# Second layer of the MLP: sixteen pairs in the seven block products, and row tiles finished as their products end

## The chip, the core and the metric

The kernel runs on one core of a Trainium2 chip. Its engines work side by side: TensorE (PE) multiplies matrices into the accumulators (PSUM), VectorE (DVE) and ScalarE (ACT) work element by element on PSUM and SBUF, GpSimd (POOL) does the same on SBUF, and SyncE (SP) issues the DMAs between SBUF and the chip's DRAM. Each engine takes its instructions in a fixed order and waits at semaphores. The metric is the time of one execution in device microseconds (us); lower is better.

## What is computed

One residual block over 1024 rows of 1024 columns: attention branches, and then an MLP with 4096 inner columns. The change lies in the MLP, and within it in the product with `w_down` and what follows.

```python
h = rms_norm(x, g_pre_mlp[l])
u = jnp.square(jax.nn.relu(h @ w_up[l]))
x = x + rms_norm(u @ w_down[l], g_post_mlp[l])
```

All values are float32. For precision each factor of a product is split into a high part in the engine's fp32r form (`hi`, a cast on ScalarE) and the rest (`lo`, a subtract on VectorE), and each block product is three matmuls: hi x hi, hi x lo, lo x hi.

## The kernel before

**First layer (up).** `up_pair(n)`, for n = 0 to 15, makes two 128-row tiles of the transposed hidden matrix, both halves of the rows, as four blocks u11, u12, u21, u22 of 128 x 512. It uses a seven-product scheme (a Strassen-Winograd form) instead of eight products. For the second layer it then builds on GpSimd the sums S1 = u12 + u22, S2 = S1 - u11, S3 = u11 - u12, S4 = u21 - S2 (lines 818 to 821), and stores A11 (u11), A12 (u21), A22 (u22) and S1 to S4 in DRAM, through SP's queue (line 826). For the last pair, n = 15, it builds no sums and stores the four plain blocks A11, A12, A22, A21.

**Second layer (down).** Again seven products stand for eight. `STORED` names their left factors in order: A11, S1, S2, A22, S3, S4, A12; the right factors are B11, T1, T2, T4, T3, B22, B21, where T1 = B12 - B11, T2 = B22 - T1, T4 = T2 - B21 and T3 = B22 - B12 are made on GpSimd by `sub` (line 862) from blocks of `w_down`. A product runs over PP = 8 pairs of inner tiles (`pp`), each with two entries `e`; pair 7 has only one (`entries`), since the 16th up pair is left out of the scheme. For a pair, `load_a` and `load_b` fetch the two factors, `parts_of` splits them (lines 607 and 608), and 24 matmuls (2 entries, 4 row tiles `t`, 3 terms) of line 898 add them into four banks. After the last pair each bank is added or copied into `lower[t]`, `upper[t]` or `p5s` (lines 902 to 924): `lower` becomes rows 0 to 3, `upper` rows 4 to 7.

**Last step.** The 16th up pair is then multiplied in the ordinary way for all eight row tiles (the `dn` matmuls of line 949, 12 for a tile). Each tile's two halves are added to its total (line 955), the tile's mean square is taken (line 108), 1 / root made by two small GpSimd operations (lines 114 or 116, and 117), the gain row `g_post2` multiplied (line 962, on GpSimd for six tiles and on VectorE for two), the residual `xf` added (line 965), and the two halves of the row are stored (line 966).

**Buffers and order.** Each tile has a tag with a fixed number of buffers; a new tile waits until an older one of its tag is no longer used. Four tags matter: `w` (four buffers of 128 x 1024, made by `wide`: u1 and u2 of an up pair, which hold u11, u12 and u21, u22; us12 and us34, which hold S1 to S4; and t1 of pairs 0 to 3, the differences T1, later T2), `row` (four; blocks of `w_down`, and before the change also the last step's `xf` and `of`), `page` (24; the hi and lo parts, four for a pair, so six pairs) and `big` (16; at first the split h blocks of the up layer, then the totals and t1 of pairs 4 to 7). A planner orders each engine's instructions ahead of the run, by program order and by when it reckons their inputs ready, so that loads and splits run ahead of PE as far as the buffers allow. PSUM has eight banks, two for each name in `BANKS`.

Of the kernel before, what the change touches and what calls it, by code (L numbers as in the profile page):

```python
# [41 lines left out]
def hybrid_block_kernel(  # L42
# [67 lines left out]
    def rstd_of(ms, pool, name):  # L110
# [22 lines left out]

    s_dram = {
        name: [dram.tile([P, 2, HALF], F32, name=f"s_dram{name}{i}") for i in range(NF // 4)]
        for name in ("A11", "A12", "A21", "A22", "S1", "S2", "S3", "S4")
    }
    bias_dram = dram.tile([N_DIFF, NREL], F32, name="bias_dram")
    bias_rows = dram.tile([N_DIFF, P, NREL], F32, name="bias_rows")
# [450 lines left out]
    def pair_page(name, dt=F32R):  # L590
        return page(name, [P, 2, HALF], dt)

    def wide(name, dt=F32):

        return stream.tile([P, 2, HALF], dt, tag="w", name=name, bufs=4)
# [10 lines left out]
    def split(hi, lo, raw):  # L606
        nc.scalar.copy(hi, raw)  # L607
        nc.vector.tensor_tensor(lo, raw, f32(hi), op=ALU.subtract)  # L608
# [159 lines left out]
    def up_pair(n):  # L768
# [43 lines left out]
        relu2(u21, u21)  # L812

        parts = {"A11": u11, "A12": u21, "A22": u22}
        if n < UP - 1:
            us12, us34 = wide(f"us12_{n}"), wide(f"us34_{n}")
            s1, s2, s3, s4 = us12[:, 0, :], us12[:, 1, :], us34[:, 0, :], us34[:, 1, :]
            nc.gpsimd.tensor_tensor(s1, u12, u22, op=ALU.add)  # L818
            nc.gpsimd.tensor_tensor(s2, s1, u11, op=ALU.subtract)
            nc.gpsimd.tensor_tensor(s3, u11, u12, op=ALU.subtract)  # L820
            nc.gpsimd.tensor_tensor(s4, u21, s2, op=ALU.subtract)
            parts |= {"S1": s1, "S2": s2, "S3": s3, "S4": s4}
        else:
            parts["A21"] = u12
        for name, part in parts.items():
            nc.sync.dma_start(out=s_dram[name][n // 2][:, n % 2, :], in_=part)

# [5 lines left out]


    PP = UP // 2
    wd = w_down.rearrange("(pp e j p) (k d) -> j k pp p e d", e=2, j=2, p=P, k=2)
    lower, upper, p5s, chain = [], [], [], []

    def entries(pp):
        return 2 if pp < PP - 1 else 1  # L840

    def load_a(name, pp):
        raw = raw_tile(f"{name}_{pp}", [P, 2, HALF])
        n = entries(pp)
        nc.sync.dma_start(out=raw[:, :n, :], in_=s_dram[name][pp][:, :n, :])
        return raw

    def load_b(j, k, pp, name):
        raw = row(f"b{j}{k}_{name}_{pp}", [P, 2, HALF])
        n = entries(pp)  # L850
        nc.sync.dma_start(out=raw[:, :n, :], in_=wd[j, k, pp, :, :n, :])
        return raw

    def parts_of(raw, name, pp):
        n = entries(pp)
        hi, lo = pair_page(f"{name}_hi{pp}"), pair_page(f"{name}_lo{pp}")
        split(hi[:, :n, :], lo[:, :n, :], raw[:, :n, :])
        return hi, lo

    def sub(out, in0, in1, pp):  # L860
        n = entries(pp)
        nc.gpsimd.tensor_tensor(out[:, :n, :], in0[:, :n, :], in1[:, :n, :], op=ALU.subtract)

    def right(name, pp):

        if name == "B11":
            b11, b12 = load_b(0, 0, pp, "a"), load_b(0, 1, pp, "a")
            t1 = wide(f"t1_{pp}") if pp < 4 else big.tile([P, 2, HALF], F32, tag="big", name=f"t1_{pp}")
            sub(t1, b12, b11, pp)
            chain.append(t1)  # L870
            return b11
        if name == "T1":
            return chain[pp]
        if name == "T2":
            sub(chain[pp], load_b(1, 1, pp, "b"), chain[pp], pp)
            return chain[pp]
        if name == "T4":
            b21 = load_b(1, 0, pp, "c")
            sub(b21, chain[pp], b21, pp)
            return b21  # L880
        if name == "T3":
            b22, b12 = load_b(1, 1, pp, "d"), load_b(0, 1, pp, "d")
            sub(b12, b22, b12, pp)
            return b12
        if name == "B22":
            return load_b(1, 1, pp, "e")
        return load_b(1, 0, pp, "f")

    for left, other in zip(STORED, ("B11", "T1", "T2", "T4", "T3", "B22", "B21")):
        accs = [bank(BANKS[t], f"d{left}_{t}") for t in range(4)]  # L890
        for pp in range(PP):
            a_hi, a_lo = parts_of(load_a(left, pp), f"l{left}", pp)
            b_hi, b_lo = parts_of(right(other, pp), f"r{other}", pp)
            for e in range(entries(pp)):
                for t in range(4):
                    ts = slice(t * P, (t + 1) * P)
                    for i, (st, mv) in enumerate(((a_hi, b_hi), (a_hi, b_lo), (a_lo, b_hi))):
                        nc.tensor.matmul(  # L898
                            accs[t], st[:, e, ts], mv[:, e, :],
                            start=(pp == 0 and e == 0 and i == 0), stop=(pp == PP - 1 and i == 2),  # L900
                        )
        for t in range(4):
            if left == "A11":
                lower.append(big.tile([P, 2, HALF], F32, tag="big", name=f"lower{t}"))
                nc.scalar.copy(lower[t][:, 0, :], accs[t])
            elif left == "S1":
                if t % 2 == 0:
                    p5s.append(big.tile([P, 2, HALF], F32, tag="big", name=f"p5_{t}"))
                nc.scalar.copy(p5s[t // 2][:, t % 2, :], accs[t])
            elif left == "S2":  # L910
                nc.vector.tensor_tensor(lower[t][:, 1, :], accs[t], lower[t][:, 0, :], op=ALU.add)
            elif left == "A22":
                upper.append(big.tile([P, 2, HALF], F32, tag="big", name=f"upper{t}"))
                nc.scalar.copy(upper[t][:, 0, :], accs[t])
            elif left == "S3":
                v, q, p4, p5 = lower[t][:, 1, :], upper[t][:, 1, :], upper[t][:, 0, :], p5s[t // 2][:, t % 2, :]
                nc.vector.tensor_tensor(q, accs[t], v, op=ALU.add)
                nc.gpsimd.tensor_tensor(p4, q, p4, op=ALU.subtract)
                nc.gpsimd.tensor_tensor(q, q, p5, op=ALU.add)
                nc.gpsimd.tensor_tensor(v, v, p5, op=ALU.add)  # L920
            elif left == "S4":
                nc.vector.tensor_tensor(lower[t][:, 1, :], accs[t], lower[t][:, 1, :], op=ALU.add)
            else:
                nc.vector.tensor_tensor(lower[t][:, 0, :], accs[t], lower[t][:, 0, :], op=ALU.add)


    g_post2 = load_row(2, big.tile([P, D], F32, tag="big", name="grow2"))
    last_a, last_b = [], []
    for j in range(2):
        raw = raw_tile(f"last_a{j}", [P, 2, HALF])  # L930
        for i in range(2):
            nc.sync.dma_start(out=raw[:, i, :], in_=s_dram[f"A{i + 1}{j + 1}"][PP - 1][:, 1, :])
        parts = pair_page(f"last_a_hi{j}"), pair_page(f"last_a_lo{j}")
        split(*parts, raw)
        last_a.append(parts)
        raw = row(f"last_b{j}", [P, 2, HALF])
        f = NF - 2 + j
        nc.sync.dma_start(out=raw, in_=w_down[f * P:(f + 1) * P, :].rearrange("p (k d) -> p k d", k=2))
        parts = pair_page(f"last_b_hi{j}"), pair_page(f"last_b_lo{j}")
        split(*parts, raw)  # L940
        last_b.append(parts)
    for i, t in enumerate((4, 5, 6, 7, 0, 1, 2, 3)):
        c, ts = t // 4, slice((t % 4) * P, (t % 4 + 1) * P)
        accs = [bank(BANKS[(2 * i + n) % 4], f"dn_{t}_{n}") for n in range(2)]
        for j in range(2):
            (a_hi, a_lo), (b_hi, b_lo) = last_a[j], last_b[j]
            for p, (st, mv) in enumerate(((a_hi, b_hi), (a_hi, b_lo), (a_lo, b_hi))):
                for n in range(2):
                    nc.tensor.matmul(  # L949
                        accs[n], st[:, c, ts], mv[:, n, :],  # L950
                        start=(j == 0 and p == 0), stop=(j == 1 and p == 2),
                    )
        tot = (upper if c else lower)[t % 4]
        for n in range(2):
            nc.vector.tensor_tensor(tot[:, n, :], accs[n], tot[:, n, :], op=ALU.add)
        tot = tot.rearrange("p a b -> p (a b)")
        xt, o = row(f"xf_{t}"), row(f"of_{t}")
        nc.sync.dma_start(out=xt, in_=x2_dram[t * P:(t + 1) * P, :])
        s2 = pb.tile([P, 1], F32, tag="ssq1", name=f"sf2_{t}", bufs=4)
        mean_square(tot, o, s2)  # L960
        r = rstd_of([s2], pb, f"f{t}")
        (nc.vector if i > 5 else nc.gpsimd).tensor_tensor(tot, tot, g_post2, op=ALU.mult)
        for n in range(2):
            ns = slice(n * HALF, (n + 1) * HALF)
            nc.vector.scalar_tensor_tensor(o[:, ns], tot[:, ns], r, xt[:, ns], op0=ALU.mult, op1=ALU.add)  # L965
            nc.sync.dma_start(out=out[t * P:(t + 1) * P, ns], in_=o[:, ns])


# [48 lines left out]
```

## Time and profile before

| | us |
|---|---|
| median of 3 runs (1511.29 to 1513.62) | 1512.61 |
| the profiled execution | 1511.9 |
| its span, first to last instruction | 1510.2 |
| PE busy | 1442.4 (96%) |
| VectorE busy | 950.0 (63%) |
| ScalarE busy | 740.0 (49%) |
| GpSimd busy | 421.2 (28%) |

The busy times are those of the profiled execution, as shares of its span. Matmuls overlap in the engine, and a busy PE is not PE at its peak: the spacing of the starts tells the rate. The granted clock of TensorE is given as a share of 2.4 GHz; 0.5 is its lower level, 1.2 GHz. The chain of waits follows the work that ended last back from the end, at each step to what released it. In a timeline, the time in brackets is how long the engine had stood idle, and what ended it.

### The profile page before, as it was taken

To read this page: it belongs to the slowest core of one execution; us is meant where nothing else is said; L and a number is where in the kernel's file an instruction comes from. 1 tells how busy PE (TensorE), PEld (TensorE's weight loads), DVE (VectorE), ACT (ScalarE), POOL (GpSimd) and SP (SyncE) were. 2 spreads that over 40 slices of the span, in tenths; PEclk is the share of its full clock that TensorE was granted. 3 is DMA by queue.
4 is the path that set the end of the run, shared out by engine and by line. 5 is a ranking of instruction groups with operands and counts; after the bars stand their busy time and mean duration, and the time that the engine had idled before them with its cause. 6 is when DMAs were issued, how large, how long until landed. Compare 5 with 4: busy or idle time off the path is not lost. (4 is left out here: it accounts for less than half of the span.)

```text
span 1510.2 us, 20192 instructions
## 1 busy us (share of the span) xinstructions
PE 1442.4 (96%) x7314; PEld 1224.7 (81%) x7314; DVE 950.0 (63%) x1384; ACT 740.0 (49%) x1326; POOL 421.2 (28%) x382
## 2 busy tenths in 40 slices
PE   7999999999999999999999749999999999999993
PEld 6888998898889888888888538788888888888882
DVE  5478988898687857445544464444444587556526
ACT  6456766665565545843334433454445345344311
POOL 2022322220000000000011256766654563434205
PEclk9999999999999999999999869999999999999997
DMA  5332223121332253644367534444446775677615
GB/s 199 88 117 65 69 54 87 56 67 57 105 84 64 77 195 112 216 140 167 112 197 222 187 104 155 153 163 158 160 156 212 251 249 169 206 243 245 201 41 195
DMA packets 94411, 218.93 MB, mean 145 GB/s; under 512 B 9340, under 2 KB 25960, under 8 KB 94312
## 3 DMA queue, kind: packets, MB, share of 16 engines
q1 hardware_dynamic: 94312, 217.66, 44.9%
q8 instruction: 57, 0.93, 0.3%
q14 instruction: 42, 0.34, 0.1%
HBM read 151.28 MB, written 60.31 MB: 140 GB/s over the span
## 5 line engine op out<-in xcount | busy, mean ns | idle before, releaser
L198 PE MATMUL acc_gate<-h_hi,lo_gate 128*128 128x512 f32 x256 | 101.0, 394 | 0.0
L196 PE MATMUL acc_gate<-h_hi,hi_gate 128*128 128x512 f32 x256 | 100.9, 394 | 0.0
L197 PE MATMUL acc_gate<-h_lo,hi_gate 128*128 128x512 f32 x256 | 100.8, 394 | 0.0
L331 DVE TENSOR_TENSOR_SCAN rest<-rest 128x896 f32<-128x896 f32 (+3 forms) x64 | 87.6, 1373 | 20.6 <-POOL rest L326 20.3
L608 DVE TENSOR_TENSOR w_lo<-ws,w_hi 128x1024 fp32r<-128x1024 f32 x32 | 44.9, 1405 | 73.6 <-ACT w_hi L607 64.2
L326 POOL TENSOR_SCALAR_AFFINE_SELECT rest<-rest 128x128 f32<-128x128 f32 x64 | 23.5, 368 | 240.7 <-ACT rest L322 236.3
L608 DVE TENSOR_TENSOR lS_lo<-raw_S,lS_hi 128x1024 fp32r<-128x1024 f32 (+1 forms) x32 | 51.7, 1616 | 38.3 <-ACT lS_hi L607 38.3
L116 POOL TENSOR_SCALAR rstd_o<-s 128x1 f32<-128x1 f32 x8 | 2.8, 354 | 249.1 <-DMA xr<-in_x_dram 211.7
L607 ACT CAST lS_hi<-raw_S 128x1024 fp32r<-128x1024 f32 (+1 forms) x32 | 32.0, 1001 | 79.4 <-DMA raw_S<-s_dramS 43.6
L898 PE MATMUL dS<-rT_hi,lS_lo 128*128 128x512 f32 x180 | 70.0, 389 | 0.0
L898 PE MATMUL dS<-rT_lo,lS_hi 128*128 128x512 f32 x180 | 70.0, 389 | 0.0
L898 PE MATMUL dS<-rT_hi,lS_hi 128*128 128x512 f32 x180 | 70.0, 389 | 0.0
L567 PE MATMUL mix<-y,hi_mix 128*128 128x512 f32 x256 | 68.6, 389 | 0.0
L607 ACT CAST w_hi<-ws 128x1024 fp32r<-128x1024 f32 x32 | 33.5, 1046 | 69.8 <-POOL ws L773 60.9
L394 ACT ACTIVATE s<-s,low 128x896 f32<-128x896 f32 (+7 forms) x64 | 49.7, 777 | 29.7 <-DVE low L389 29.5
L375 POOL MEMSET bias<- 64x64 f32 x4 | 0.6, 144 | 214.4 <-DMA bias<-bias_rows 214.4
L389 DVE CUSTOM_DVE_ANT_0 s<-z,bias 128x512 f32<-128x512 f32 (+3 forms) x64 | 37.0, 586 | 32.4 <-PE z L263 26.6
L723 ACT ACTIVATE u<-u 128x512 f32<-128x512 f32 x48 | 30.2, 630 | 54.8 <-DVE u L802 33.7
L567 PEld LDWEIGHTS mix<-y,hi_mix 128*128 128x128 f32 x256 | 48.0, 188 | 10.0
L198 PEld LDWEIGHTS acc_gate<-h_hi,lo_gate 128*128 128x128 f32 x256 | 48.2, 188 | 9.2
L197 PEld LDWEIGHTS acc_gate<-h_lo,hi_gate 128*128 128x128 f32 x256 | 48.2, 188 | 8.8
L608 DVE TENSOR_TENSOR lA_lo<-raw_A,lA_hi 128x1024 fp32r<-128x1024 f32 (+1 forms) x24 | 35.5, 1478 | 31.4 <-ACT lA_hi L607 30.9
(341 smaller groups left out, 4896.9 us busy)
## 6 DMA issues: line engine op xcount, KB each, us to landing
raw_up<-in_w_up_dram SPq DMA_DIRECT2D x32, 512.0 KB, 3.9
s_dramS<-us SPq DMA_DIRECT2D x60, 256.0 KB, 2.0
raw_S<-s_dramS SPq DMA_DIRECT2D x28, 512.0 KB, 4.5
s_dramA<-u SPq DMA_DIRECT2D x49, 256.0 KB, 3.1
raw_A<-s_dramA SPq DMA_DIRECT2D x21, 512.0 KB, 3.7
raw_gate<-in_w_in_dram SPq DMA_DIRECT2D x16, 512.0 KB, 3.7
gate_dram<-gt SPq DMA_DIRECT2D x32, 256.0 KB, 2.5
y<-y_dram SPq DMA_DIRECT2D x16, 512.0 KB, 6.1
```

The costliest lines, as they stand in the source:

```text
L196: nc.tensor.matmul(acc, w_hi[:, ks], h_hi[k][:, cs], start=(k == 0), stop=False)
L197: nc.tensor.matmul(acc, w_hi[:, ks], h_lo[k][:, cs], start=False, stop=False)
L198: nc.tensor.matmul(acc, w_lo[:, ks], h_hi[k][:, cs], start=False, stop=(k == NK - 1))
L326: nc.gpsimd.affine_select(tl[:, dg], tl[:, dg], pattern=[[-1, P]], compare_op=ALU.is_gt, fill=fill, base=0, channel_multiplier=1,)
L331: nc.vector.tensor_tensor_scan(back, back, back, 1.0, op0=ALU.mult, op1=ALU.bypass)
L389: nc.vector.tensor_tensor_reduce(out=s[:, c0:c1], in0=z, in1=bias[:, S - nk + c0:S - nk + c1], scale=1.0, scalar=BIG if prev is None else ...
L394: e = nc.scalar.activation(s[:, :nk], s[:, :nk], AF.Exp, bias=low, scale=-1.0, accum_out=sums[:, m:m + 1],)
L567: nc.tensor.matmul(accs[i][c], st[:, ks], mv[:, cs], start=(first and k % 4 == 0), stop=(last and k % 4 == 3),)
L607: nc.scalar.copy(hi, raw)
L608: nc.vector.tensor_tensor(lo, raw, f32(hi), op=ALU.subtract)
L723: nc.scalar.activation(dst, src, AF.Relu)
L898: nc.tensor.matmul(accs[t], st[:, e, ts], mv[:, e, :], start=(pp == 0 and e == 0 and i == 0), stop=(pp == PP - 1 and i == 2),)
```

## The change

For the last up pair the sums S1 to S4 are made and stored like all others, and A21 is no longer stored. Every pair of the second layer has two entries. The separate last product is gone. The row tiles are finished where their products end: `evict` of S3 finishes rows 4 to 7 (`begin_rows`, `half_rows`, `end_rows`), that of S4 squares and scales the second half of rows 0 to 3, and that of A12 the first half, and ends them. In the last product, A12, pairs 0 to 3 run as before, while the factors of pairs 4 to 7 are kept, and their matmuls run tile by tile: 24 for tile 0, then its `evict`, and so on. The gain is multiplied in halves on VectorE for all tiles. `xf` and `of` are of tag `big`, and the gain row is loaded before the products. The core of the diff, without the removed last step, without `load_a`, `load_b` and `right`, which only lose their `entries`, and without the evictions that only change their form:

```diff
@@ up_pair
         parts = {"A11": u11, "A12": u21, "A22": u22}
-        if n < UP - 1:
-            us12, us34 = wide(f"us12_{n}"), wide(f"us34_{n}")
...
-        else:
-            parts["A21"] = u12
+        us12, us34 = wide(f"us12_{n}"), wide(f"us34_{n}")
+        s1, s2, s3, s4 = us12[:, 0, :], us12[:, 1, :], us34[:, 0, :], us34[:, 1, :]
+        nc.gpsimd.tensor_tensor(s1, u12, u22, op=ALU.add)
+        nc.gpsimd.tensor_tensor(s2, s1, u11, op=ALU.subtract)
+        nc.gpsimd.tensor_tensor(s3, u11, u12, op=ALU.subtract)
+        nc.gpsimd.tensor_tensor(s4, u21, s2, op=ALU.subtract)
+        parts |= {"S1": s1, "S2": s2, "S3": s3, "S4": s4}
         for name, part in parts.items():
             nc.sync.dma_start(out=s_dram[name][n // 2][:, n % 2, :], in_=part)
@@ second layer
     PP = UP // 2
+    BY_TILE = 4
-    def entries(pp):
-        return 2 if pp < PP - 1 else 1
...
+    def accumulate(acc, factors, t, first, last):
+        (a_hi, a_lo), (b_hi, b_lo) = factors
+        ts = slice(t * P, (t + 1) * P)
+        for e in range(2):
+            for i, (st, mv) in enumerate(((a_hi, b_hi), (a_hi, b_lo), (a_lo, b_hi))):
+                nc.tensor.matmul(
+                    acc, st[:, e, ts], mv[:, e, :], start=(first and e == 0 and i == 0), stop=(last and e == 1 and i == 2)
+                )
+
+    g_post2 = load_row(2, big_f32("grow2").rearrange("p a b -> p (a b)"))
+    pending = {}
+
+    def begin_rows(t, tot):
+        xt, o = big_f32(f"xf_{t}"), big_f32(f"of_{t}")
+        nc.sync.dma_start(out=xt.rearrange("p a b -> p (a b)"), in_=x2_dram[t * P:(t + 1) * P, :])
+        s2 = pb.tile([P, 2], F32, tag="ssq", name=f"sf2_{t}", bufs=4)
+        pending[t] = tot, xt, o, s2
+
+    def half_rows(t, n):
+        tot, xt, o, s2 = pending[t]
+        mean_square(tot[:, n, :], o[:, n, :], s2[:, n:n + 1])
+        nc.vector.tensor_tensor(tot[:, n, :], tot[:, n, :], g_post2[:, n * HALF:(n + 1) * HALF], op=ALU.mult)
+
+    def end_rows(t):
+        tot, xt, o, s2 = pending[t]
+        r = rstd_of([s2[:, 0:1], s2[:, 1:2]], pb, f"f{t}")
+        for n in range(2):
+            nc.vector.scalar_tensor_tensor(o[:, n, :], tot[:, n, :], r, xt[:, n, :], op0=ALU.mult, op1=ALU.add)
+            nc.sync.dma_start(out=out[t * P:(t + 1) * P, n * HALF:(n + 1) * HALF], in_=o[:, n, :])
+
+    def evict(left, t, acc):
...
+        elif left == "S3":
+            v, q, p4, p5 = lower[t][:, 1, :], upper[t][:, 1, :], upper[t][:, 0, :], p5s[t // 2][:, t % 2, :]
+            nc.vector.tensor_tensor(q, acc, v, op=ALU.add)
+            nc.gpsimd.tensor_tensor(p4, q, p4, op=ALU.subtract)
+            nc.gpsimd.tensor_tensor(q, q, p5, op=ALU.add)
+            nc.gpsimd.tensor_tensor(v, v, p5, op=ALU.add)
+            begin_rows(4 + t, upper[t])
+            for n in range(2):
+                half_rows(4 + t, n)
+            end_rows(4 + t)
+        elif left == "S4":
+            nc.vector.tensor_tensor(lower[t][:, 1, :], acc, lower[t][:, 1, :], op=ALU.add)
+            begin_rows(t, lower[t])
+            half_rows(t, 1)
+        else:
+            nc.vector.tensor_tensor(lower[t][:, 0, :], acc, lower[t][:, 0, :], op=ALU.add)
+            half_rows(t, 0)
+            end_rows(t)
+
     for left, other in zip(STORED, ("B11", "T1", "T2", "T4", "T3", "B22", "B21")):
         accs = [bank(BANKS[t], f"d{left}_{t}") for t in range(4)]
+        together = PP - BY_TILE if left == "A12" else PP
+        kept = []
         for pp in range(PP):
...
+            factors = parts_of(load_a(left, pp), f"l{left}", pp), parts_of(right(other, pp), f"r{other}", pp)
+            if pp >= together:
+                kept.append(factors)
+                continue
+            for t in range(4):
+                accumulate(accs[t], factors, t, pp == 0, pp == PP - 1)
         for t in range(4):
...
+            for i, factors in enumerate(kept):
+                accumulate(accs[t], factors, t, False, i == len(kept) - 1)
+            evict(left, t, accs[t])
...
-    for i, t in enumerate((4, 5, 6, 7, 0, 1, 2, 3)):
...
```

## Rows read from the trace of the kernel before

**Rows 1.** The page's head.

```profile
span 1510.2 us, 20192 instructions
```

**Rows 2.** Chain of waits, second layer: start, us, engine, name, line, instructions.

```profile
1179.60 40.12 PE dA L898 x177
...
1342.12 81.60 PE dS L898 x360
1423.72 40.80 PE dA L898 x180
1464.52 7.95 PE dn L949 x35
```

**Rows 3.** Timeline of PE, its last instructions: start, us, line, operation, count.

```profile
1485.66 0.61 PE L949 MATMUL dn<-last_b_hi,last_a_lo 128*128 128x512 f32 x2
```

**Rows 4.** Groups by line and shape, 760 to 1511: busy us, mean ns | idle before.

```profile
L108 ACT ACTIVATE or<-o 128x512 f32<-128x512 f32 x16 | 9.5, 600 | 7.2 <-PE o L656 4.5 <-DMA x_dram<-xr 2.7
...
L117 POOL TENSOR_TENSOR rstd_o<-rstd_o,neg_half 128x1 f32<-128x1 f32 x8 | 4.5, 560 | 0.6
...
L108 ACT ACTIVATION_READ_ACCUMULATOR or<-o 128x1 f32 x16 | 3.2, 203 | 0.0
L116 POOL TENSOR_SCALAR rstd_o<-s 128x1 f32<-128x1 f32 x8 | 2.8, 354 | 249.1 <-DMA xr<-in_x_dram 211.7 <-ACT or L108 37.2
L924 DVE TENSOR_TENSOR lower<-dA,lower 128x512 f32<-128x512 f32 x4 | 2.7, 691 | 13.8 <-PE dA L898 13.8
```

**Rows 5.** Timeline of VectorE, its last operations.

```profile
1505.82 1.41 DVE L965 SCALAR_TENSOR_TENSOR of<-lower,rstd_f,xf 128x512 f32<-128x512 f32 x2 [0.77 <-POOL rstd_f L117]
```

**Rows 6.** Timeline of GpSimd from up pair 13's sums to the first t1.

```profile
1146.44 1.29 POOL L818 TENSOR_TENSOR us<-u,u 128x512 f32<-128x512 f32 x1 [1.78 <-ACT u L724]
...
1150.31 1.29 POOL L821 TENSOR_TENSOR us<-u,us 128x512 f32<-128x512 f32 x1
1164.05 1.28 POOL L818 TENSOR_TENSOR us<-u,u 128x512 f32<-128x512 f32 x1 [12.46 <-ACT u L724]
...
1168.94 2.15 POOL L821 TENSOR_TENSOR us<-u,us 128x512 f32<-128x512 f32 x1
1173.30 4.75 POOL L862 TENSOR_TENSOR t<-b_a,b_a 128x1024 f32<-128x1024 f32 x2 [2.20 <-DMA s_dramS<-us]
```

**Rows 7.** Timelines of SP, VectorE and ScalarE, from the first loads to pair 2.

```profile
1138.54 0.39 SPq L851 DMA_DIRECT2D b_a<-in_w_down_dram  x1
...
1161.57 0.68 DVE L808 TENSOR_TENSOR u<-p_av,v 128x512 f32<-128x512 f32 x1
...
1175.74 3.21 SPq L851 DMA_DIRECT2D b_a<-in_w_down_dram  x4
...
1179.69 0.69 DVE L808 TENSOR_TENSOR u<-p_av,v 128x512 f32<-128x512 f32 x1 [2.08 <-PE p_av L717]
...
1181.40 1.05 ACT L607 CAST rB_hi<-b_a 128x1024 fp32r<-128x1024 f32 x1 [2.46 <-DMA b_a<-in_w_down_dram]
...
1182.48 1.22 DVE L608 TENSOR_TENSOR rB_lo<-b_a,rB_hi 128x1024 fp32r<-128x1024 f32 x1 [2.10 <-ACT rB_hi L607]
...
1185.41 0.63 ACT L724 ACTIVATE u<-u 128x512 f32<-128x512 f32 x1
```

**Rows 8.** Busy us (x instructions) by engine, granted clock (PEclk), DMA, in three stretches.

```profile
860.00:862.00 2.00, 0.00 (x0) 0.00 (x0) 2.00 (x2) 2.00 (x4) 2.00 (x2) 0.54 0.00 0
1383.00:1424.00 41.00, 41.00 (x182) 33.96 (x181) 27.62 (x21) 15.38 (x17) 22.50 (x12) 1.00 0.62 192
1491.00:1492.00 1.00, 0.00 (x0) 0.00 (x0) 0.30 (x1) 0.21 (x2) 0.63 (x2) 0.82 0.98 361
```

**Rows 9.** Timeline of PE where it starts again after its long gap.

```profile
888.10 0.79 PE L717 MATMUL p_sc<-hT_hi,w_hi 128*128 128x512 f32 x1 [30.03 <-ACT w_hi L607]
...
894.32 0.39 PE L717 MATMUL p_sc<-hT_hi,w_lo 128*128 128x512 f32 x1
```

**Rows 10.** Timeline of all engines where S3's banks are evicted: a split for S4.

```profile
1382.73 1.06 ACT L607 CAST lS_hi<-raw_S 128x1024 fp32r<-128x1024 f32 x1 [0.71 <-PE dS L898]
```

More of the change, by code (lines that the diff above doesn't have):

```diff
@@ L135, in hybrid_block_kernel @@
         name: [dram.tile([P, 2, HALF], F32, name=f"s_dram{name}{i}") for i in range(NF // 4)]
-        for name in ("A11", "A12", "A21", "A22", "S1", "S2", "S3", "S4")
+        for name in ("A11", "A12", "A22", "S1", "S2", "S3", "S4")
     }
@@ L814, in up_pair @@
         parts = {"A11": u11, "A12": u21, "A22": u22}
-        if n < UP - 1:
-            us12, us34 = wide(f"us12_{n}"), wide(f"us34_{n}")
[L817 to L822, printed above, removed]
-        else:
-            parts["A21"] = u12
+        us12, us34 = wide(f"us12_{n}"), wide(f"us34_{n}")
[5 more added lines that the diff above has]
+        parts |= {"S1": s1, "S2": s2, "S3": s3, "S4": s4}
         for name, part in parts.items():
@@ L835, in hybrid_block_kernel @@
     PP = UP // 2
+    BY_TILE = 4
     wd = w_down.rearrange("(pp e j p) (k d) -> j k pp p e d", e=2, j=2, p=P, k=2)
     lower, upper, p5s, chain = [], [], [], []
-    def entries(pp):
-        return 2 if pp < PP - 1 else 1
     def load_a(name, pp):
         raw = raw_tile(f"{name}_{pp}", [P, 2, HALF])
-        n = entries(pp)
-        nc.sync.dma_start(out=raw[:, :n, :], in_=s_dram[name][pp][:, :n, :])
+        nc.sync.dma_start(out=raw, in_=s_dram[name][pp])
         return raw
@@ L849, in load_b, with sub, big_f32 @@
         raw = row(f"b{j}{k}_{name}_{pp}", [P, 2, HALF])
-        n = entries(pp)
-        nc.sync.dma_start(out=raw[:, :n, :], in_=wd[j, k, pp, :, :n, :])
+        nc.sync.dma_start(out=raw, in_=wd[j, k, pp])
         return raw
     def parts_of(raw, name, pp):
-        n = entries(pp)
         hi, lo = pair_page(f"{name}_hi{pp}"), pair_page(f"{name}_lo{pp}")
-        split(hi[:, :n, :], lo[:, :n, :], raw[:, :n, :])
+        split(hi, lo, raw)
         return hi, lo
-    def sub(out, in0, in1, pp):
-        n = entries(pp)
-        nc.gpsimd.tensor_tensor(out[:, :n, :], in0[:, :n, :], in1[:, :n, :], op=ALU.subtract)
+    def sub(out, in0, in1):
+        nc.gpsimd.tensor_tensor(out, in0, in1, op=ALU.subtract)
+    def big_f32(name):
+        return big.tile([P, 2, HALF], F32, tag="big", name=name)
     def right(name, pp):
@@ L867, in right @@
             b11, b12 = load_b(0, 0, pp, "a"), load_b(0, 1, pp, "a")
-            t1 = wide(f"t1_{pp}") if pp < 4 else big.tile([P, 2, HALF], F32, tag="big", name=f"t1_{pp}")
-            sub(t1, b12, b11, pp)
+            t1 = wide(f"t1_{pp}") if pp < 4 else big_f32(f"t1_{pp}")
+            sub(t1, b12, b11)
             chain.append(t1)
@@ L874, in right @@
         if name == "T2":
-            sub(chain[pp], load_b(1, 1, pp, "b"), chain[pp], pp)
+            sub(chain[pp], load_b(1, 1, pp, "b"), chain[pp])
             return chain[pp]
@@ L878, in right @@
             b21 = load_b(1, 0, pp, "c")
-            sub(b21, chain[pp], b21, pp)
+            sub(b21, chain[pp], b21)
             return b21
@@ L882, in right @@
             b22, b12 = load_b(1, 1, pp, "d"), load_b(0, 1, pp, "d")
-            sub(b12, b22, b12, pp)
+            sub(b12, b22, b12)
             return b12
@@ new lines, in end_rows @@
+    def end_rows(t):
[5 more added lines that the diff above has]
+    def evict(left, t, acc):
+        if left == "A11":
+            lower.append(big_f32(f"lower{t}"))
+            nc.scalar.copy(lower[t][:, 0, :], acc)
+        elif left == "S1":
+            if t % 2 == 0:
+                p5s.append(big_f32(f"p5_{t}"))
+            nc.scalar.copy(p5s[t // 2][:, t % 2, :], acc)
+        elif left == "S2":
+            nc.vector.tensor_tensor(lower[t][:, 1, :], acc, lower[t][:, 0, :], op=ALU.add)
+        elif left == "A22":
+            upper.append(big_f32(f"upper{t}"))
+            nc.scalar.copy(upper[t][:, 0, :], acc)
+        elif left == "S3":
[16 more added lines that the diff above has]
+            end_rows(t)
@@ L889, in hybrid_block_kernel @@
     for left, other in zip(STORED, ("B11", "T1", "T2", "T4", "T3", "B22", "B21")):
         accs = [bank(BANKS[t], f"d{left}_{t}") for t in range(4)]
+        together = PP - BY_TILE if left == "A12" else PP
+        kept = []
         for pp in range(PP):
[L892 to L901, printed above, removed]
@@ L902, in hybrid_block_kernel @@
-        for t in range(4):
[L903 to L924, printed above, removed]
@@ L927, in hybrid_block_kernel @@
[L927 to L941, printed above, removed]
@@ L942, in hybrid_block_kernel @@
-    for i, t in enumerate((4, 5, 6, 7, 0, 1, 2, 3)):
[L943 to L966, printed above, removed]
```

## The prediction

> **What bounds the kernel now.** I read the page first: in its slices of the span of 1510.2 us [rows 1] TensorE (PE) is full nearly everywhere, so an edit counts only if it removes matmuls or moves the ends of PE's work. The second view is the chain of waits [rows 2]. From 1179.6 us to the end of the dn matmuls of L949 the second layer is one unbroken run of PE: 177 matmuls in 40.12 us, 360 in 81.60, 180 in 40.80, so 0.2267 us for each, and no wait of PE inside. Every split (the hi cast on ScalarE, the lo subtract on VectorE), every load and every GpSimd operation of that layer is hidden. The chain leaves PE after 35 of the 96 dn matmuls. The third view, PE in order of time, ends at 1485.66 + 0.61 = 1486.3 us [rows 3]; the span ends at 1510.2 [rows 1]. The last 23.9 us are row tiles being finished one after the other on VectorE, ScalarE, GpSimd and the output DMAs. Two places matter, then: this tail, and any place where the change makes PE wait within its run.
>
> **Matmuls.** Before: 7 products x 15 entries x 12 matmuls = 1260, and 8 tiles x 12 = 96 dn matmuls: 1356. After: 7 x 16 x 12 = 1344. Twelve fewer at 0.2267 us are 2.7 us on the path, so PE would end at 1483.6.
>
> **The tail.** Rows 4 to 7 are finished behind S3, under the 81.6 us of the last two products, and half of rows 0 to 3 behind S4. In A12 the last four pairs run tile by tile, 24 matmuls or 5.4 us each, so tiles 0 to 2 end under the matmuls of the next ones. Each needs about 0.69 + 0.69 + 1.41 us of VectorE [rows 4, 5], within 5.4. Behind the last matmul stands one half row: the add 0.69, the square of 512 columns 0.60 and its accumulator 0.20, the two small GpSimd steps 0.35 and 0.56 (the gain is multiplied on VectorE beside the square and is over before them) [rows 4], then from the start of the first final operation to the end of the span 4.38 (1505.82 to 1510.2) [rows 5], with 0.3 us for the gaps between engines, an estimate from the last tile's starts. The sum is 7.1 us against 23.9 now: 16.8 us gained. Without a new wait the span would be 1483.6 + 7.1 = 1490.7.
>
> **The added wait: where the first layer hands over to the second.** The last up pair (n = 15) now also makes S1 to S4, in two more tiles of the tag "w", which has four buffers. The differences B12 - B11 (t1 of pairs 0 to 3) live in the same tag. The trace tells in which order those buffers are given. Both loads for t1 of pair 0 were issued by 1138.54 [rows 7], the sums of pair 13 ended at 1151.6 and their stores went out, which left two buffers empty; GpSimd then stood idle 12.46 us before 1164.05, yet it ran the sums of pair 14 first and t1 only at 1173.30, once the S stores of pair 14 had landed [rows 6]. So a tag's buffers go out in program order. Before, t1 of pairs 0 and 1 got the two buffers that pair 14's sums left. After, pair 15's sums take these, and t1 of pair 0 has to wait until u11 and u12 of pair 15 are used up, that is behind the new sums on GpSimd.
>
> Step by step: the last product of the up layer releases VectorE's add for u12 at 1179.69. In the pair before, GpSimd's first sum followed that add by 2.5 us (1161.57 to 1164.05), some 0.5 of it a copy that pair 15 has not: 1181.7 [rows 6, 7]. From the first sum to the end of the fourth it is 5.16 us with VectorE quiet (1146.44 to 1151.60) and 7.04 beside its subtracts (1164.05 to 1171.09) [rows 6]; I take 5.2, since VectorE has no second-layer pair to split then, so 1186.9. The first t1 takes 2.4 (4.75 for two) [rows 6]: 1189.3. Only that frees the rows of B11 and B12 of pair 0 (tag "row", four buffers), for which the loads of pair 2 wait. Before, the loads went out at 1175.74, the cast began at 1181.40 and the lo part was there at 1182.48 + 1.22 = 1183.7 [rows 7]: 8.0 us behind t1. After, two loads instead of four go first, so I take 7.4: pair 2 is ready at 1196.7. PE wants it after pairs 0 and 1, 45 matmuls behind 1179.60, at 1189.8 [rows 2]. **PE waits about 7 us** where it had 6 to spare. The bounds: 5.5 (all of it quiet, and the load and split 6.2: 3.7 to the quickest landing and 2.3 for cast and subtract, an estimate) to 15 (u12's square ending only at 1186.0, as it stood in ScalarE's queue before [rows 7], and 7.04, 3.3 and 8.0, which is 1204.5). Later pairs are not late: t1 of pair 1 follows 2.4 us on, and each round of loads and t1 serves two pairs, 10.9 us of PE.
>
> The clock adds to it. In the one long gap that PE has late in the kernel the granted clock fell to half within 2 us (0.54 in 860 to 862 [rows 8]), and from the restart at 888.10 thirteen matmuls took until 894.32, 6.2 us instead of 2.9 [rows 9]: 3 us lost. Behind the last matmul, ended at 1486.3, it fell only in 1491 to 1492 [rows 8], about 5 us on; a wait of 7 exceeds that too. I add 3 us; the bounds are 0 and 3. The Trainium skill, "TensorE: Matmul & The Clock Gate", Part 1, has the slow clock as the default that activity lifts, which speaks against any edit that opens a gap in a full PE; by it, too, the wait costs more than its length, and the rows agree.
>
> Together the wait costs 10 us (5.5 to 18).
>
> **What else moves.** Full second entries of pair 7: seven products with 2 casts of 1.05 instead of 0.62 us, 2 subtracts of about 1.2 instead of 0.7, and 512 more columns for four GpSimd differences. They get 2.7 us more PE time per product to hide in and come last in it: nothing. SP issues three more stores for pair 15 (seven for four) and the gain row's load early; behind them stand loads which wait for t1 anyway: nothing beyond the above. Its output DMAs of rows 4 to 7 now stand among the loads for S4 and A12, and wait on VectorE there. At 1382.73 S4's pair 5 was being split while S3 ended [rows 10], so five pairs, 27 us of PE, are ready ahead. In S4's 41 us VectorE is busy 27.6 us, GpSimd 22.5 and ScalarE 15.4 [rows 8]. The four rows add 8 multiplications at 0.69 and 8 final operations at 0.7, 11.1 us, within the 13.4 left. Beside GpSimd, operations there take up to twice as long (1.29 against 2.15 for one sum [rows 6]); then it is 22 us, 9 over what is left, which the lead of 27 takes. The Trainium skill, "SBUF — State Buffer", "Who interferes with whom", calls this an exclusive lock between a VectorE operation with two SBUF inputs and GpSimd's reads; by it the six gain multiplications moved from GpSimd to VectorE don't relieve the shared port, and the sum here would be the 22, not the 11. Either way PE is not reached. ScalarE's 8 half squares (6.4 us) fit in 41 - 15.4.
>
> **How the numbers follow.** The profiled execution took 1511.9 us for its span of 1510.2; the median of the runs shown is 0.7 above it. A time is thus the span + 2.4. Likeliest: 1490.7 + 10 + 2.4 = 1503.
>
> **Rivals.** First, no new wait: the buffers go out otherwise than I read them, or t1 finds another one. For it: only the order on one queue shows the rule. Then 1493. Chance 0.22; the forecast has 0.60. Second, the wait at its high end of 18: 1511, chance 0.10, which is nearly no change. Third, slower: VectorE's in-order queue behind S3. Row 4 needs three GpSimd sums, row 7 all twelve (22.5 us of GpSimd). If the row operations stand ahead of the splits of S4's pairs 5 to 7, pair 5 is split at 1382.9 + 22.5 + 22 + 2.4 = 1429.8, while PE wants it at 1382.9 + 27.2 = 1410.1: a wait of 20 us, and 3 for the clock: 1526. It decides from the point where rows and sums together hold VectorE over 27 us. Against it: now S4's splits stand between S3's evictions [rows 10]. Chance 0.08. That row tiles are not finished early, because their order in the queues puts them behind everything, is within this one.
>
> The range is from 1491.5, the first rival with 1.5 us off for a tail shorter than summed, to 1511, the second; it leaves out about 0.15. A measurement of this kernel can tell about 0.2%, 3 us, from no change. Faster than 1509.6: 0.60 + 0.22 + a little of the second = 0.84; within: 0.08; slower: 0.08.
>
> **What would show it.** Right: a gap of PE of 6 to 8 us near 1190, at A11's third pair, put down to a cast or subtract of rB that follows a load of b_a, with the granted clock at half behind it; GpSimd's first t1 behind four sums of pair 15; an unbroken run of PE from there; 7 us between the last matmul and the end. Wrong: no gap there (then 1493), or a gap in S4 or A12, or a tail of over 10 us.

## The result and the profile after

The changed kernel takes 1501.7 us (median of 4 runs, 1499.0 to 1502.8) where the kernel before takes 1512.0 beside it: the ratio is 0.993, with a 95% interval of 0.991 to 0.995. It is faster by about 10 us. The forecast was 1503.0, with a range of 1491.5 to 1511.0.

The profiled execution took 1501.75 us. The page's head, which answers to [rows 1]:

```profile
span 1500.0 us, 20132 instructions
```

The chain of waits (start, us, what), from the last up product to the end. It answers to [rows 2].

```profile
1178.85 2.73 PE p_av L717 x12
...
1181.66 0.70 DVE u L808
...
1183.05 0.64 ACT u L724
...
1183.82 1.28 POOL us L817
...
1188.92 2.41 POOL t L853
...
1191.35 3.61 DMA b_a<-in_w_down_dram
...
1194.98 1.05 ACT rB_hi L607
...
1196.07 35.25 PE dA L888 x144
1231.32 87.04 PE dS L888 x384
1318.36 43.52 PE dA L888 x192
1361.88 87.04 PE dS L888 x384
1448.92 43.53 PE dA L888 x192
...
1492.48 0.70 DVE lower L943
...
1494.02 0.79 POOL rstd_f L116
...
1495.50 0.75 DVE of L912
```

Before, the chain ran through PE alone from 1179.60 on. Now it makes one detour, from the last up product through VectorE, ScalarE, four sums of GpSimd, the first t1, a load and a cast; only then does PE go on. From 1196.07 to 1492.45 PE runs without a break. The view of PE's waits, from 1000 us to the end (what ended them; us in total, times, longest), has this one row:

```profile
PE dA L888 <- ACT rB_hi L607: 4.3, 1, 4.3
```

PE's timeline around that wait; the second row is the first work of A11's pair 2:

```profile
1191.38 0.39 PE L888 MATMUL dA<-rB_hi,lA_lo 128*128 128x512 f32 x1
1196.07 2.08 PE L888 MATMUL dA<-rB_hi,lA_hi 128*128 128x512 f32 x4 [4.31 <-ACT rB_hi L607]
...
1200.93 0.46 PE L888 MATMUL dA<-rB_hi,lA_hi 128*128 128x512 f32 x1
1201.23 0.40 PE L888 MATMUL dA<-rB_lo,lA_hi 128*128 128x512 f32 x1
```

And PE's busy time, the granted clock, the DMA share and GB/s in stretches there:

```profile
1185.00:1190.00 5.00, 5.00 (x23) 1.00 0.44 171
1190.00:1195.00 5.00, 1.77 (x8) 0.92 0.63 205
1195.00:1200.00 5.00, 3.93 (x9) 0.50 0.72 253
1200.00:1202.00 2.00, 2.00 (x8) 0.74 0.36 33
1202.00:1210.00 8.00, 8.00 (x37) 1.00 0.93 329
```

PE stood still for 4.3 us, came back at 1.2 GHz, and was at 2.4 GHz again from about 1201.

**Where the time went.** In a clean run the stretch from A11's first matmul to S1's first is 46.41 us before (1173.31 to 1219.72 = 1179.60 + 40.12 [rows 2]) and 49.13 with the twelve added matmuls of A11. It is 56.03 now (1175.29 to 1231.32), so the wait cost 6.9 us: 4.3 of standing and 2.6 behind it. The tail is 1500.0 - 1492.45 = 7.55 us instead of 23.9. A11 also began 2.0 us later (1175.29 against 1173.31), though the change lies behind it. The attention's z matmuls, at the kernel's beginning, already start at 67.87 instead of 65.20, but that alone doesn't explain it: in the experiment without a product by row tile they start at 65.10, and A11 still at 1175.61. A11's start differs from one profiled execution to another (below). The sum is 1510.2 - 2.7 (matmuls) - 16.35 (tail) + 6.9 (wait) + 2.0 = 1500.05, which is the span.

### The profile page after: what moved, and what is told of

It reads as the page before. It is cut to its first block, busy times and chain, and to the rows that moved or that the text cites. A ratio compares the mean times of both kernels' runs of the same rounds, so it can differ in the third digit from the quotient of the medians.

```text
span 1500.0 us, 20132 instructions
## 1 busy us (share of the span) xinstructions
PE 1444.2 (96%) x7302; PEld 1224.6 (82%) x7302; DVE 961.2 (64%) x1378; ACT 743.9 (50%) x1338; POOL 418.4 (28%) x380
## 5 line engine op out<-in xcount | busy, mean ns | idle before, releaser
L608 DVE TENSOR_TENSOR lS_lo<-raw_S,lS_hi 128x1024 fp32r<-128x1024 f32 x32 | 59.0, 1843 | 39.3 <-ACT lS_hi L607 39.3
L888 PE MATMUL dS<-rT_hi,lS_hi 128*128 128x512 f32 x192 | 74.7, 389 | 0.0
L888 PE MATMUL dS<-rT_lo,lS_hi 128*128 128x512 f32 x192 | 74.7, 389 | 0.0
L888 PE MATMUL dS<-rT_hi,lS_lo 128*128 128x512 f32 x192 | 74.7, 389 | 0.0
L607 ACT CAST lS_hi<-raw_S 128x1024 fp32r<-128x1024 f32 x32 | 33.7, 1053 | 78.0 <-DMA raw_S<-s_dramS 45.9
L196 PEld LDWEIGHTS acc_gate<-h_hi,hi_gate 128*128 128x128 f32 x256 | 48.2, 188 | 8.6
```

Source lines behind the costliest of these rows:

```text
L196: nc.tensor.matmul(acc, w_hi[:, ks], h_hi[k][:, cs], start=(k == 0), stop=False)
L888: nc.tensor.matmul(acc, st[:, e, ts], mv[:, e, :], start=(first and e == 0 and i == 0), stop=(last and e == 1 and i == 2))
```

## Experiments

All are edits of the changed kernel. The runs of the kernel before beside them had a median of 1512.0.

**Every t1 in the tag big.** The differences of pairs 0 to 3 leave the tag w, for which the new sums compete.

```diff
-            t1 = wide(f"t1_{pp}") if pp < 4 else big_f32(f"t1_{pp}")
+            t1 = big_f32(f"t1_{pp}")
```

> One edit to the changed kernel: t1 of pairs 0 to 3 lives in a buffer of the tag big, not w; the sums of up pair 15, their stores and all else stay. Theory (PE's gap at A11's third pair comes from t1 waiting for a buffer of w): GpSimd runs the first t1 well before the sums of pair 15, the loads of pair 2 go out early, PE has no gap there and the clock stays at 2.4 GHz; the 4.3 us of gap and the 2.6 us of slow matmuls behind it are gone, 1501.7 - 6.9 = 1494.8 us. Rival 1 (the four added sums and three added stores themselves hold up GpSimd and the DMAs, whatever the buffer): a gap of 3 to 4 us stays, 1500 to 1502. Rival 2 (the gap goes, but the second layer's supply is late again a pair or two on): a gap at pair 4 or 5 of 2 to 4 us, 1498 to 1500.

It took 1493.7 us (1492.9 to 1495.6), ratio 0.988 (0.987 to 0.990). GpSimd's timeline:

```profile
1162.17 4.95 POOL L853 TENSOR_TENSOR t<-b_a,b_a 128x1024 f32<-128x1024 f32 x2 [9.88 <-PE c L717]
1167.08 1.28 POOL L817 TENSOR_TENSOR us<-u,u 128x512 f32<-128x512 f32 x1
...
1187.96 1.30 POOL L817 TENSOR_TENSOR us<-u,u 128x512 f32<-128x512 f32 x1
```

The first two differences now run at 1162, ahead of the sums of pair 14 (1167.08), and the sums of pair 15 come at 1187.96, when nobody waits for them. The chain of waits stays on PE:

```profile
1180.44 42.84 PE dA L888 x189
1223.29 87.04 PE dS L888 x384
```

From A11's first matmul (1174.16) to 1223.29 are 49.13 us, the clean figure, and the view of PE's waits has no row from 1000 us on, so the supply isn't late at a later pair either. All sums and stores of pair 15 are still there, so the wait is one for a buffer and not the cost of the added work. Against the changed kernel the median falls by 8.0 us: 6.9 for the wait, and A11 begins 1.1 earlier in this execution.

**Only the sums of pair 15 in big.** The converse: t1 stays in w, and the two tiles that crowd it out leave.

```diff
-        us12, us34 = wide(f"us12_{n}"), wide(f"us34_{n}")
+        if n < UP - 1:
+            us12, us34 = wide(f"us12_{n}"), wide(f"us34_{n}")
+        else:
+            us12, us34 = (big.tile([P, 2, HALF], F32, tag="big", name=f"us{i}_{n}") for i in ("12", "34"))
```

> Only the four sums of up pair 15 are put into two buffers of the tag big; all differences t1 stay in the tag w. It asks what the wait is made of: that the sums of pair 15 exist and run (work of GpSimd ahead of t1), or only that they take the two buffers of w which t1 of pairs 0 and 1 had before the change. By the theory (the buffers' order) the sums of pair 14 free the two buffers for t1 again, t1 of pair 0 runs ahead of the sums of pair 15, at about 1173, and there is no gap at A11's third pair. The differences of pairs 2 and 3 then wait for the last two buffers of up pair 15, used until the sums end near 1187 and are stored near 1190: t1 of pair 2 ends near 1192, and the pair that loads into its rows (pair 4) is ready at 1199 to 1200, where PE wants it at 1202. So the time is that of the run with every t1 in big, 1494 to 1495, or up to 3 us more if pair 4 comes late. By the rival (the sums themselves, their work and stores, hold the first difference up) the gap of 4 us stays and the time is 1501.7.

It took 1495.1 us (1494.2 to 1498.5); the profiled execution is the longest of the four, 1498.5. GpSimd's timeline:

```profile
1171.89 2.15 POOL L823 TENSOR_TENSOR us<-u,us 128x512 f32<-128x512 f32 x1
1175.35 4.77 POOL L856 TENSOR_TENSOR t<-b_a,b_a 128x1024 f32<-128x1024 f32 x2 [1.30 <-DMA s_dramS<-us]
1188.47 1.80 POOL L820 TENSOR_TENSOR us<-u,u 128x512 f32<-128x512 f32 x1 [8.35 <-ACT u L724]
...
1195.07 4.73 POOL L856 TENSOR_TENSOR t<-b_a,b_a 128x1024 f32<-128x1024 f32 x2
```

The first t1 is back behind the stores of pair 14, as in [rows 6], and the gap at pair 2 is gone. The next two come behind the sums of pair 15, which are later than expected (1188.47; VectorE and ScalarE split pairs 2 and 3 first). Pairs 4 and 5 are thus each short of a lo part once, as the view of PE's waits has it (us in total, times, longest):

```profile
PE dA L891 <- DVE rB_lo L608: 1.7, 2, 0.9
```

The stretch from A11 to S1 is 51.81 us (1176.26 to 1228.07), 2.7 over the clean one. By the medians the run is only 1.4 slower than the one with every t1 in big; whether the three shorter executions had these waits isn't known. So the buffers' order is the cause, and the same rule then bites, weakly, two pairs later.

**The gap filled with matmuls that nobody reads.** Twenty matmuls behind A11's second pair hold PE busy while it waits; the wait itself stays.

```diff
+            if left == "A11" and pp == 1:
+                idle = bank("acc", "idle")
+                (a_hi, a_lo), (b_hi, b_lo) = factors
+                for i in range(20):
+                    nc.tensor.matmul(idle, a_hi[:, 0, 0:P], b_hi[:, 0, :], start=(i == 0), stop=(i == 19))
```

> The changed kernel with 20 matmuls of 0.227 us that nobody reads put into PE's gap (behind A11's second pair): it computes nothing else. Theory (4.3 us of the loss is the wait, a further 2.6 us the slow clock behind it): the granted clock stays at 1.00 from 1185 to 1210, A11's remaining 144 matmuls take 32.6 us instead of 35.3, and the time falls to about 1499. Rival (the matmuls behind the gap are slow because their factors come late, not because of the clock): they take 35 us again and the time stays at 1501.7 or rises a little.

A single run took 1500.8 us, its span 1499.0. That is within the changed kernel's 1499.0 to 1502.8, so only the trace can tell. PE's timeline:

```profile
1190.94 4.69 PE L962 MATMUL idle<-rB_hi,lA_hi 128*128 128x512 f32 x20
1195.77 1.20 PE L888 MATMUL dA<-rB_hi,lA_hi 128*128 128x512 f32 x4
...
1203.70 0.50 PE L888 MATMUL dA<-rB_lo,lA_hi 128*128 128x512 f32 x1 [0.90 <-DVE rB_lo L608]
```

Its busy time and granted clock in the stretch where the changed kernel had 0.50:

```profile
1195.00:1200.00 5.00, 4.80 (x20) 1.00 0.60 218
```

The clock stays at 2.4 GHz, so its fall does come from the standing. But little is won: the 144 matmuls from pair 2 on take 34.5 us (1195.77 to 1230.29) instead of 35.25, where 144 x 0.2267 is 32.6. At full clock PE now runs out of lo parts: the first 28 of the 144 take 7.93 us (1195.77 to 1203.70) where 28 x 0.2267 is 6.35. VectorE's timeline shows why:

```profile
1195.74 1.22 DVE L608 TENSOR_TENSOR rB_lo<-b_a,rB_hi 128x1024 fp32r<-128x1024 f32 x1 [14.06 <-ACT rB_hi L607]
1196.89 3.42 DVE L608 TENSOR_TENSOR lA_lo<-raw_A,lA_hi 128x1024 fp32r<-128x1024 f32 x1
1200.23 3.41 DVE L608 TENSOR_TENSOR rB_lo<-b_a,rB_hi 128x1024 fp32r<-128x1024 f32 x1
```

Two of the three subtracts take 3.4 us, beside GpSimd's differences of pairs 2 and 3, which run from 1196.13 on. Of the 2.6 us that the changed kernel loses behind its gap, the slow clock by itself is thus worth 0.7, by this one run; the other 1.9 would be lost to late factors anyway. My theory was too large by a factor of almost four, and the rival was the nearer one.

**No product by row tile.** `BY_TILE` from 4 to 0: A12's four tiles all end with the last pair.

> The changed kernel with all pairs of the last product run together (BY_TILE 0), so that the four last tiles end within the last 18 matmuls (4.1 us). Theory (tile by tile is worth what VectorE's 2.8 us a tile can't hide): four tiles queue up, 11.2 us of VectorE from 4.1 us before PE's end, the tail grows from 7.6 to about 12 us, and the time to about 1506. Rival (the early finishing of rows 4 to 7 alone makes the tail, the order in the last product does nothing): 1501.7. PE's gap at A11 stays in either case.

It took 1504.8 us (1504.0 to 1505.6), 3.1 more than the changed kernel. A12 begins at 1449.66 and its 192 matmuls end at 1493.19, so the tail is 10.6 us. The theory was right in kind, its 12 us for the tail and 1506 for the time somewhat too much; the rival fell. GpSimd's timeline, the first row tile's step and the last one's, shows what the queue does beside making tiles wait:

```profile
1490.69 0.30 POOL L116 TENSOR_SCALAR rstd_f<-sf 128x1 f32<-128x1 f32 x1 [57.54 <-ACT of L108]
...
1496.44 1.16 POOL L116 TENSOR_SCALAR rstd_f<-sf 128x1 f32<-128x1 f32 x1 [0.73 <-ACT of L108]
```

VectorE's timeline has what ran beside them:

```profile
1490.50 0.69 DVE L943 TENSOR_TENSOR lower<-dA,lower 128x512 f32<-128x512 f32 x1 [0.67 <-PE dA L888]
...
1496.11 2.06 DVE L912 SCALAR_TENSOR_TENSOR of<-lower,rstd_f,xf 128x512 f32<-128x512 f32 x3
```

The small step of one column takes 0.30 us for the first tile, beside an add that reads PSUM and one SBUF tile, and 1.16 for the last, beside final operations that read two SBUF tiles.

**The last two pairs by row tile.** `BY_TILE` from 4 to 2.

> Of the last product the last two pairs instead of the last four are multiplied tile by tile, so a tile ends 2.7 us after the one before it instead of 5.4. A tile's finishing takes VectorE 0.69 + 0.69 + 1.41 = 2.8 us, about one tile's matmuls. By the theory (the tail is VectorE's queue of unfinished tiles plus one tile's own chain of 7.5) the queue behind the last matmul is 3 x 0.1 to 3 x 0.3 us: tail 7.9 to 8.5, time 1502 to 1502.7, beside 1504.8 with no tile by tile and 1501.7 with four pairs. By the rival (a tile's own chain through ScalarE and GpSimd, about 4 us until its last operation, sets the pace in queue order, so that tiles 2.7 us apart pile up) the tail is 10 us and the time 1504.

It took 1502.9 us (1501.2 to 1506.7). The tail of the profiled execution is 9.15 us (A12 from 1446.82, so its end at 1490.35, and a span of 1499.5): 1.6 more than with four, between what the two theories gave. VectorE's timeline:

```profile
1489.58 1.42 DVE L912 SCALAR_TENSOR_TENSOR of<-lower,rstd_f,xf 128x512 f32<-128x512 f32 x2 [0.24 <-POOL rstd_f L117]
...
1491.52 0.68 DVE L943 TENSOR_TENSOR lower<-dA,lower 128x512 f32<-128x512 f32 x1
```

With tiles 2.7 us apart they pile up: the add of the last tile starts 1.2 us after the last matmul, because the final operations of the second tile and the multiplication of the third stand before it in VectorE's queue. Its small step takes 1.16 again. The time is 1.2 more by the medians, less than the runs of either kernel differ among themselves.

**Rows 4 to 7 finished late.** The four lines that finish row 4 + t move from `evict` of S3 to that of A12, behind row t.

```diff
         elif left == "S3":
...
-            begin_rows(4 + t, upper[t])
-            for n in range(2):
-                half_rows(4 + t, n)
-            end_rows(4 + t)
...
             half_rows(t, 0)
             end_rows(t)
+            begin_rows(4 + t, upper[t])
+            for n in range(2):
+                half_rows(4 + t, n)
+            end_rows(4 + t)
```

> One part of the change undone: rows 4 to 7 are no longer finished behind the product S3, but each behind one of the row tiles 0 to 3 in the last product. The rest is as in the changed kernel. By the theory, finishing them under S4's matmuls is what takes them out of the tail: moved back, VectorE has 0.69 + 0.69 + 1.41 for row t and 1.38 + 1.41 for row 4 + t, 5.6 us for each 5.4 us of matmuls, and behind the last matmul stands row 7 as well as row 3: two squares (1.4 us on ScalarE), two multiplications and two final operations more, 2.5 to 4 us: tail 10 to 11.5, time 1504 to 1506. The wait at A11's third pair stays, and the splits in S4 keep their lead of 27 us. By the rival (the last product has room for all eight rows, so it doesn't matter that rows 4 to 7 are early) the time is 1501.7.

It took 1509.1 us (median of 10 runs, 1506.3 to 1514.3), 7.4 more than the changed kernel and hardly less than the kernel before. The tail is 1508.4 - 1493.84 = 14.6 us, twice that of the changed kernel and over my 10 to 11.5. VectorE's timeline, the add of the last tile:

```profile
1498.12 0.68 DVE L939 TENSOR_TENSOR lower<-dA,lower 128x512 f32<-128x512 f32 x1
```

That add stands behind the row operations of earlier tiles and starts 4.3 us after its last matmul. I had counted VectorE's busy time for a slot (5.6 us for 5.4) and left out its waits: from 1477 to 1490, while tiles end, it is busy for 7.5 us of 13, and then has no idle time until 1498. It waits for the rows' steps on ScalarE and GpSimd, and ScalarE in its turn for buffers: the square writes its unread output to `of`, a tile of big, and on ScalarE's timeline row 4's first square waits until row 0 is stored and gives a buffer back.

```profile
1484.59 0.63 ACT L108 ACTIVATE of<-upper 128x512 f32<-128x512 f32 x1 [1.86 <-DMA out_dram<-of]
```

Two such waits come to 4.1 us; the changed kernel has none. So the 7.4 us are not the price of the late work alone: a part that was not measured by itself comes from the buffers of big.

**t1 in big, and the gain's multiplication out of place.** Besides the first edit, the square's unread output goes to a scratch tile and the multiplication writes `o` instead of the total, so that it need not wait for the square.

```diff
-        mean_square(tot[:, n, :], o[:, n, :], s2[:, n:n + 1])
-        nc.vector.tensor_tensor(tot[:, n, :], tot[:, n, :], g_post2[:, n * HALF:(n + 1) * HALF], op=ALU.mult)
+        mean_square(tot[:, n, :], tmp_tile(f"sq_{t}_{n}"), s2[:, n:n + 1])
+        nc.vector.tensor_tensor(o[:, n, :], tot[:, n, :], g_post2[:, n * HALF:(n + 1) * HALF], op=ALU.mult)
...
-            nc.vector.scalar_tensor_tensor(o[:, n, :], tot[:, n, :], r, xt[:, n, :], op0=ALU.mult, op1=ALU.add)
+            nc.vector.scalar_tensor_tensor(o[:, n, :], o[:, n, :], r, xt[:, n, :], op0=ALU.mult, op1=ALU.add)
```

> The changed kernel with t1 in big, and with the gain's product written to another tile than the row total, so that it need not wait for the square's reading of that total. Theory: the gap and the slow clock go (6.9 us), and in the tail the first small GpSimd step is no longer beside the multiplication, 0.35 instead of 0.79 us: 1501.7 - 6.9 - 0.4 = 1494.4. Rival (that step is slow for another reason, or the multiplication's wait is not on the total): as with t1 in big alone, 1494.8, and the step still takes 0.8 us.

It took 1494.4 us (1493.7 to 1494.7), the same, within the spread, as with t1 in big alone. The trace does show the step. First VectorE's timeline of the changed kernel, where the multiplication of the last half row waits for the square:

```profile
1493.96 0.69 DVE L906 TENSOR_TENSOR lower<-lower,grow 128x512 f32<-128x512 f32 x1 [0.79 <-ACT of L108]
```

and that of this kernel, where it follows the add (at 1485.84) at once:

```profile
1486.56 0.69 DVE L906 TENSOR_TENSOR of<-lower,grow 128x512 f32<-128x512 f32 x1
```

In this kernel's chain of waits GpSimd's step is short again:

```profile
1487.44 0.30 POOL rstd_f L116
```

The tail is 7.19 us (1485.81 to 1493.0) instead of 7.59 with t1 in big alone. A gain of 0.4 is below what the times can tell.

## Why the prediction was right

**What bounds the kernel.** Right: PE's run and its ends decide. Three of the experiments changed only how the rows are finished, and each moved the time by about what it moved the tail (3.05 and 3.1, 1.6 and 1.2, 7.0 and 7.4; of these the 1.2 is within the spread of the runs).

**Matmuls.** Right: 192 in 43.53 us are 0.2267 each, as before.

**The tail.** 7.55 us against 7.1. The step that failed is that the gain's multiplication is "over before" the small GpSimd steps. It works in place on the total, which the square still reads. So it starts at 1493.96, beside GpSimd's first step at 1494.02, and this takes 0.79 instead of the 0.35 of [rows 4], a mean over the steps of another stage (`rstd_o`). That is the missing 0.4; with the multiplication written to another tile, the step takes 0.30. The last row tiles of the kernel before already showed both the wait for the square and the long step, on VectorE's and on GpSimd's timeline:

```profile
1503.83 1.23 DVE L962 TENSOR_TENSOR lower<-lower,grow 128x1024 f32<-128x1024 f32 x1 [0.76 <-ACT of L108]
```

```profile
1491.29 0.23 POOL L114 TENSOR_SCALAR rstd_f<-sf 128x1 f32<-128x1 f32 x1 [3.29 <-ACT of L108]
...
1503.88 1.26 POOL L114 TENSOR_SCALAR rstd_f<-sf 128x1 f32<-128x1 f32 x1 [2.27 <-ACT of L108]
```

The small step took 0.23 us while VectorE stood idle, and 1.26 beside the multiplication. That rows 4 to 7 are hidden behind S3 is a larger part of the gain than the sum made plain: moving them back costs 7.4 us (in part for want of buffers), and giving up the product by row tile 3.1.

**The added wait.** The mechanism was right, at the pair, in the order and with the buffers that were named; both experiments on the buffers bear it out. From u12's add to the end of the first t1 it is 9.7 us (1181.66 to 1191.33), predicted 9.6 (1179.69 to 1189.3). The mis-sized term is the last: from there to PE's start it is 4.7 us and not 7.4. The load landed in 3.6 us, and PE needs only the cast of 1.05. PE begins with the four hi x hi matmuls of the tiles (the row "x4" above), before the lo part is there, while I let it wait for both. So the gap is 4.3 us, below my lower bound of 5.5 for it.

**The clock.** 2.6 us lost behind the gap, against 3 in the sum. The size was right, and that was in part luck, for the cause holds only for a smaller share: the filled gap shows that 0.7 is the clock's and the rest late factors, which the slow clock happens to cover. The 3 us read from [rows 9] mixed the two already: there the matmuls start 0.43 us apart at the lower clock (889.12 and 889.54), which is 5.5 us for the thirteen, and the rest of the 6.2 is waiting between them. The Trainium skill, "TensorE: Matmul & The Clock Gate", Part 1, has the slow clock as the default that activity lifts; the rows agree (0.50 behind the gap, 1.00 with it filled). How much more than its length a gap costs depends here on whether the factors are there.

**What else moves.** Right that S4 absorbs the row work: there is no wait of PE in it, and the rival with VectorE's queue behind S3 (1526 us) fell. It used up part of the cover, though. VectorE's busy time behind S3's end, by engine, in 42 us (PE, PEld, DVE, ACT, POOL, clock, DMA):

```profile
1406.00:1448.00 42.00, 42.00 (x187) 34.79 (x186) 34.60 (x31) 18.06 (x28) 25.69 (x19) 1.00 0.76 261
```

27.6 of 41 us before [rows 8], 34.6 of 42 now. The last split of S4, on VectorE's timeline, stands at

```profile
1428.18 1.21 DVE L608 TENSOR_TENSOR rB_lo<-b_e,rB_hi 128x1024 fp32r<-128x1024 f32 x1
```

and PE wanted it at 1448.92 - 5.44 = 1443.5: a lead of 14 us. Without the row operations in S4, with rows 4 to 7 finished late, the same split stands at

```profile
1420.07 2.31 DVE L608 TENSOR_TENSOR rB_lo<-b_e,rB_hi 128x1024 fp32r<-128x1024 f32 x1
```

and was wanted at 1444.9, a lead of 22.5. So the rows took 8.4 us of the lead, close to the 9 of the prediction's dearer case (22 us of work for 13.4 left). But the lead itself was smaller than the 27 it counted with at S3's end. The row operations did not stand ahead of the splits but among them.

**The sum.** 1503.1 - 3.1 (wait) + 0.45 (tail) + 2.0 (A11's later start) - 0.65 (1.75 us around the span instead of 2.4) = 1501.8. So the forecast was off by 1.3 us because an error of 3.1 and a shift of 2.0 that nothing predicted went against each other; that it came so close is luck. The first rival's price was right as well: with the wait away, the time is 1493.7 where it gave 1493; only its condition did not hold.

**The faster version.** With every t1 in big, the kernel takes 1493.7 us, 1.2% less than the kernel before.

## What to carry to other kernels

Where a change makes more tiles of a tag, list who else lives in that tag and in which order its buffers are handed out: here two more tiles in w held up the first operation of the next stage, at 6.9 us, and moving that stage's tiles to a tag with free buffers gave all of it back. For a tail, count each row tile's chain through the other engines, and the buffers that it holds, and not only the busy time of the busiest engine, and finish tiles where PE still has work of another product. Before costing a wait, look which operand the first instruction behind it reads.

## What was not expected of the hardware

- A GpSimd step on one column takes 0.30 us with VectorE idle (the last row tile, with the multiplication out of place), 0.79 beside the gain's multiplication in the changed kernel, and 1.16 for the last tile with no product by row tile. It is not always so: with two pairs by row tile one such step took 0.31 (at 1490.19) while VectorE was at its final operations without a break.
- VectorE's subtract of 1024 columns takes 1.22 us alone and 3.4 when GpSimd's difference of 1024 columns (2.4 alone) runs beside it: about the sum of the two. The Trainium skill, "SBUF — State Buffer", "Who interferes with whom", has an exclusive lock between a VectorE operation with two SBUF inputs and GpSimd's reads; these rows agree.
- Where A11 begins differs by up to 3.9 us between kernels whose code is the same up to there: 1172.98 with two pairs by row tile, 1174.62 with the gap filled, 1175.29 in the changed kernel, 1175.61 with none by row tile, 1176.92 with rows 4 to 7 late. What sets it was not tried. It limits what one profiled execution can tell to about this size; stretches within a trace can be compared far more closely.
